# A decoder layer on one core: thirteen 8 KB buffers kept in one pool to the end, norm inputs fetched at step 60, and VectorE's hi and lo parts interleaved in the branch stage

## The chip, the cores and the metric

The kernel runs on one core of a Trainium2 chip. The metric is the device time of one execution in microseconds (us), as the median of several runs. TensorE (PE) multiplies, VectorE (DVE) and ScalarE (ACT) do elementwise work, GpSimd (POOL) does a little of it, and SyncE (SP) issues most DMAs.

## The reference

One decoder layer, on x of 512 tokens by 1024 channels, all in float32. Cut to what matters:

```python
proj = x @ w_in                       # q, k, v (3 groups x 8 heads x 64), ssm input, gate logits
q, k = apply_rope(q), apply_rope(k)
attn = merge of three windowed causal attentions, weighted by their softmax denominators
y_attn = attn @ w_attn_br
y_s = s5_ssm(u, ...)                  # complex diagonal state space model
glu = gelu(y_s) @ w_glu
y_ssm = (glu[:, :512] * sigmoid(glu[:, 512:])) @ w_ssm_br
mixed = sigmoid(gate0) * y_attn + sigmoid(gate1) * y_ssm
h = layer_norm(2 ** 0.25 * x + mixed @ w_out)
ff = (silu(h @ w_ff_gate) * (h @ w_ff_up)) @ w_ff_down
out = layer_norm(2 ** 0.25 * h + ff)
```

## The kernel before

Every product is made of three fp32r matmuls. An operand is split into a rounded part (hi) and the remainder (lo): `split` (line 177) has ScalarE copy the value into hi, and VectorE then subtract hi from the value to give lo. `mm3` (line 185) multiplies hi by hi, hi by lo and lo by hi (lines 186 to 188). Activations and weights are both split, each weight tile just in time.

Weights pass through the class `Weights`. SP loads units of 1 MB into two buffers `raw`; a unit holds two tiles, and `split` turns a tile into `whi` and `wlo`, three steps ahead of its use. `release`, called at the end of a step, gives that step's slot back and splits the next tile. The load of a unit is issued when the second tile of the unit two before it has been split. The second half of `w_out` (tiles 72 to 75) is not split into slots but into 8 KB buffers of its own, `w`.

The work is a list of numbered steps. Steps 0 to 55 project x and run the state space model and the attention in between (`at_step` hangs a function on a step number, `run_fill` calls it). Then come:

- GLU, steps 56 to 59: two banks of 12 matmuls each, then a tanh and a product, split into `gh`, `gl`.
- The branch stage, steps 60 to 67, counted n = 0 to 7 here: two banks per step, 24 matmuls. The banks come from a ring of four (0 to 3), so step n + 2 writes the banks that VectorE reads after step n. For n below 4 VectorE multiplies the state space branch by its gate (`gt`); from n = 4 it does so for the attention branch, adds both and splits the sum into `mix_hi`, `mix_lo`.
- `merge_pair(hp)`, at steps 58, 59, 60 and 61, for the four pairs of heads: two matmuls spread the merge weights to banks (`wb`), and VectorE forms `oa[1] * wb[1]`, then `a1 = oa[0] * wb[0]`, then their sum, which is split into `ath`, `atl`. In step 60 and 61 it stands ahead of the step's own gate products in VectorE's order. `oa[0]` is held in phase order, so that the product reads it with a stride of four elements.
- The output stage (`wo`): four token tiles by two column halves, eight weight tiles n. The first half goes over all four token tiles for each weight tile (banks 4 to 7), the second (banks 0 to 3) is done token tile by token tile. `wo_out` adds x (`xn`) and takes statistics; `normalize_shared` norms a token tile, half of its columns on VectorE and half on ScalarE and GpSimd; `turn_h` transposes it on TensorE (`hb`) and splits it into `hh`, `hl`. `turn_h(0)` stands in t = 2 after n = 5, `turn_h(1)` in t = 3 after n = 5.
- Feed forward (`fg`) and its last product (`dn`), then the second norm and the stores.

Two groups of 8 KB buffers are used. Pool `pa` has tags `big0` to `big8` and `gat0` to `gat3`, thirteen in all, given by name with `home`. It is closed after the branch stage (line 1031), together with the smaller `at` and `sa`; pool `pb` is opened over the same memory, with eleven buffers `ff` and a tile `hn`. The inputs of the norm, two halves of x (`xn`) and the scale and offset (`lnb`), 1 MB each, are loaded into `ff` buffers: `xn` at the start of the output stage, `lnb` after its second weight tile. Engines run their instructions in the order of the program, and so does SP.

Of the kernel before, what the change touches and what calls it, by code (L numbers as in the profile page):

```python
# [10 lines left out]
F32 = mybir.dt.float32  # L11
# [140 lines left out]
def emit(ctx, tc, i, out):  # L152
# [42 lines left out]
    def kslice(pair, k, cols=slice(None)):  # L195
        return pair[0][k // 4][:, k % 4, cols], pair[1][k // 4][:, k % 4, cols]

    pa_ctx = ExitStack()
    pa = pa_ctx.enter_context(tc.tile_pool(name="pa", bufs=1))
    at = pa_ctx.enter_context(tc.tile_pool(name="at", bufs=2))  # L200
    sa = pa_ctx.enter_context(tc.tile_pool(name="sa", bufs=1))

# [14 lines left out]
        return gat(n[1:], name, dt) if isinstance(n, str) else big(n, name, dt)  # L217

    w = Weights(nc, wp, split)
    w.add(None, 8)  # L220
    for n in range(2, N_GLU, 2):
        kind, g, un, _ = STEPS[n]
# [10 lines left out]
    for un in range(2):  # L233
        w.add(i["w_out"][un], 2)
    for un in range(2, 4):
        w.add(i["w_out"][un], 2, lambda name, dt: ffslot(name, dt))
    for f in range(NFF):
        w.add(i["w_gu"][f], 8)
    for f in range(NFF // 2):
# [32 lines left out]
    w.n_split = 4  # L272
    w.load()

    rope = pa.tile([P, 2, 512], F32, tag="rope", name="rope")
    masks = pa.tile([P, 512], F32, tag="masks", name="masks").rearrange("p (n k) -> p n k", n=2)
    bgate = sa.tile([P, 16], F32, name="bgate")
    prep = gat(0, "prep")
    sm = prep[:, 0:1024].rearrange("p (a r e) -> p a r e", a=2, r=2)
# [157 lines left out]
    powers(pw, lb)  # L437


    bb = pa.tile([P, 512], F32, tag="bb", name="bb").rearrange("p (r g h) -> p r g h", r=2, g=NGP)  # L440
    btmp = [zt[:, 256 * j : 256 * (j + 1)].rearrange("p (g h) -> p g h", g=NGP) for j in range(2)]
    b_raw = sm[:, 0].rearrange("p r (g h) -> p r g h", h=16)
    c_raw = sm[:, 1].rearrange("p r (g h) -> p r g h", h=16)
# [352 lines left out]
    def attn_values(kind, hp, blks):  # L796
        if blks[0] == 0:
            units["o", kind] = outs(f"o{kind}{hp}")
        ob = units["o", kind]
        for blk in blks:  # L800
            ks, tv = units.pop((kind, hp, blk))
            for c, (z, kb) in enumerate(ks):
                for hh in range(2):
                    h = 2 * hp + hh
                    pe.matmul(ob[64 * hh : 64 * hh + 64, 128 * blk : 128 * blk + 128],
                              z[2][:, kb, 64 * h : 64 * h + 64], tv[:, hh, 128 * c : 128 * c + 128],
                              start=(c == 0), stop=(c == len(ks) - 1))
        if blks[-1] == 3:
            if hp == 0:
                oa[kind] = big((6, 3)[kind], f"oa{kind}").rearrange("p (q t) -> p q t", q=4)  # L810
            act.copy(oa[kind][:, hp, :], ob)

    merged = {}

# [2 lines left out]
    def merge_near(n):  # L817

        if n == 0:
            merged["wt"] = wt = pa.tile([P, 512], F32R, tag="bb", name="wt").rearrange("p (r e) -> p r e", r=4)  # L820
            pool.memset(wt[:, :, 32:P].bitcast(F32), 0.0)
            sp.dma_start(sdr.rearrange("(b p) e -> p b e", p=P), st[0].rearrange("p b e h -> p b (e h)"))
        else:
            sp.dma_start(near_st.rearrange("p r e h -> p (r e h)"), sdr.rearrange("(c r) e -> c (r e)", r=4))

    def merge_sel():

        z = pa.tile([P, 2, 512], F32R, tag="rope", name="selr")
        for kind in range(2):
            hi, lo = (ident[:, c : c + 8].unsqueeze(2).broadcast_to([P, 8, 64]) for c in (8 * kind, 8 * kind + 16))  # L830
            tt(z[:, kind].rearrange("p (h m) -> p h m", m=64), hi, lo, ALU.add)
        merged["sel"] = z.rearrange("p k (h m) -> p k h m", h=NPAIR)
# [19 lines left out]
    def merge_turn():  # L852
        b = turned("wt")
        for r in range(4):
            pe.transpose(b[:, 128 * r : 128 * r + 128], merged["wt"][:, r].bitcast(F32), ident)

        merged["w"] = pa.tile([P, 512], F32R, tag="masks", name="whl")
        dve.tensor_copy(merged["w"], b)

    def merge_pair(hp):  # L860
        if hp == 0:
            for j, n in (("g1", "h"), (1, "l")):
                merged[n] = home(j, f"at{n}", F32R).rearrange("p (q t) -> p q t", q=4)
        wb = [pairs_(f"wb{hp}{k}") for k in range(2)]
        for kind in range(2):
            pe.matmul(wb[kind], merged["sel"][:, kind, hp, :], merged["w"], start=True, stop=True)
        tt(oa[1][:, hp, :], oa[1][:, hp, :], wb[1], ALU.mult)
        a1 = at.tile([P, 512], F32, tag="cq", name=f"a1{hp}")
        tt(by_phase(a1), as_phases(oa[0][:, hp, :]), by_phase(wb[0]), ALU.mult)
        tt(a1, a1, oa[1][:, hp, :], ALU.add)  # L870
        split(merged["h"][:, hp, :], merged["l"][:, hp, :], a1)

    gts = [None] * 4

# [61 lines left out]
    for kind in range(2):  # L936
        for j, n in enumerate(TURNS[kind]):
            if j >= 2:
                at_step(n, attn_values, kind, *pairs[j - 2])
            if j < len(pairs):  # L940
                at_step(n, attn_scores, kind, *pairs[j])
            if 0 < j <= len(pairs):
                at_step(n, attn_turn, kind, *pairs[j - 1])
    at_step(43, merge_near, 0)
    at_step(45, merge_near, 1)
    at_step(52, merge_sel)
# [38 lines left out]
    for n in range(4):  # L985
        ws = w.views[N_GLU + n]
        bs = []
        for e in range(2):
            b = glu(f"gl{n}{e}")
            co = slice(128 * e, 128 * e + 128)  # L990
            for k in range(4):
                mm3(b, (ws[0][:, k, co], ws[1][:, k, co]), (gluin["y"][0][:, k, :], gluin["y"][1][:, k, :]), k == 0, k == 3)
            bs.append(b)
        th = at.tile([P, 512], F32, tag="sw", name=f"th{n}")
        act.activation(th, bs[1], AF.Tanh, scale=0.5)
        stt(th, th, 1.0, bs[0], ALU.add, ALU.mult)
        split(gh_[:, n, :], gl_[:, n, :], th, 0.5)
        w.release()
        run_fill(N_GLU + n)
        run_fill(N_GLU + n + 0.5)  # L1000
# [3 lines left out]
    for n in range(8):  # L1004
# [11 lines left out]
        part(0, (3,))  # L1016
        run_fill(N_BR + n)
        part(1, (3,))
        for c in range(2):
            ch = 2 * (n % 4) + c  # L1020
            t0, t1 = gts[ch // 4][:, ch % 4, :], gts[2 + ch // 4][:, ch % 4, :]
            if n < 4:
                stt(t1, t1, 1.0, bs[c], ALU.add, ALU.mult)
            else:
                stt(t0, t0, 1.0, bs[c], ALU.add, ALU.mult)
                tt(t0, t0, t1, ALU.add)
                hi, lo = kslice(mx, ch)
                split(hi, lo, t0, 0.5)
        w.release()
        run_fill(N_BR + n + 0.5)  # L1030
    pa_ctx.close()
# [3 lines left out]
    bt = ctx.enter_context(tc.tile_pool(name="bt", bufs=2))  # L1035
    w.free.extend((pb, n) for n in range(3, 5))

    def ffslot(name, dt=F32):
        return pb.tile([P, 2048], dt, tag="ff", name=name, bufs=11)

    xn = [ffslot(f"xn{j}").rearrange("p (t d) -> p t d", t=2) for j in range(2)]
    lnb = ffslot("lnb").rearrange("p (e d) -> p e d", e=2)
    hn = pb.tile([P, NTT, D], F32, name="hn")
    epsb = bt.tile([P, 1], F32, name="epsb", bufs=1)
    pool.memset(epsb, -0.5)

# [29 lines left out]
        pool.tensor_tensor(z[:, hi], z[:, hi], ln[:, 1, hi], op=ALU.add)  # L1076

    bst1 = [bt.tile([P, 2, 6], F32, name=f"bsta{t}", bufs=1) for t in range(NTT)]
    hp_ = tuple([ffslot(f"h{n}{j}", F32R).rearrange("p (k t) -> p k t", k=4) for j in range(2)] for n in "hl")

    def wo_mm(d, n, t):
        ws = w.views[N_OUT + n]
# [3 lines left out]

    def wo_out(d, t, e):
        cs = slice(512 * e, 512 * e + 512)
        stt(hn[:, t, cs], xn[t // 2][:, t % 2, cs], ALPHA, d, ALU.mult, ALU.add)
        dve.bn_stats(bst1[t][:, e, :], hn[:, t, cs])  # L1090

    hturn = ring(4, 5, 6, 7)

    def turn_h(t):
        z = hn[:, t, :]
        tsl = slice(128 * t, 128 * t + 128)
        for j in range(2):
            b = hturn(f"hb{t}{j}")
# [2 lines left out]
                pe.transpose(b[:, 128 * e : 128 * e + 128], z[:, 128 * k : 128 * k + 128], ident)  # L1101
            split(hp_[0][j][:, :, tsl], hp_[1][j][:, :, tsl], b.rearrange("p (e c) -> p e c", e=4))

    for j in range(2):
        sp.dma_start(xn[j], i["x"].rearrange("(t p) d -> p t d", p=P)[:, 2 * j : 2 * j + 2, :])
    od = [bank(4 + t, f"wo0{t}") for t in range(NTT)]
    for n in range(4):
        for t in range(NTT):
            wo_mm(od[t], n, t)
        if n < 3:  # L1110
            w.release()
            if n < 2:
                w.split()
            if n == 1:
                sp.dma_start(lnb, i["ln1"].unsqueeze(0).broadcast_to([P, 2, D]))
    for t in range(NTT):
        wo_out(od[t], t, 0)
    od = [bank(t, f"wo1{t}") for t in range(NTT)]
# [2 lines left out]
    for t in range(NTT):  # L1121
        for n in range(4, 8):
            wo_mm(od[t], n, t)
            if t >= 2 and n == 5:
                turn_h(t - 2)
        if t == 3:
            normalize_shared(hn[:, 2, :], mvs[2], lnb)
        wo_out(od[t], t, 1)
        dve.bn_aggr(mvs[t][:, 0:2], bst1[t])
        rstd(mvs[t])  # L1130
        if t < 2:
            normalize_shared(hn[:, t, :], mvs[t], lnb)
            w.split()
    normalize(hn[:, 3, :], mvs[3], lnb)
    w.split()


# [10 lines left out]
    def ff_gate(f):  # L1148
        if f % 2 == 0:
            if f < 14:  # L1150
                slot = ffslot(f"ff{f // 2}", F32R)
                ffs.append(slot.rearrange("p (e c t) -> p e c t", e=2, c=2))
            else:
                slot = ap_.tile([P, 4, 512], F32R, tag="act", name=f"ff{f // 2}")
# [20 lines left out]
            w.release()  # L1175
        ff_gate(f)

    lnb2 = ffslot("lnb2").rearrange("p (e d) -> p e d", e=2)
    act.dma_start(lnb2, i["ln2"].unsqueeze(0).broadcast_to([P, 2, D]))
    out_rows = out.rearrange("(c r) d -> r c d", r=NTT)  # L1180

# [12 lines left out]
    for k in range(NFF - NLAST):  # L1194
# [1 line left out]
            for e, cs in enumerate(halves):  # L1196
                down(acc[t][e], k, t, cs, k == 0, t == NTT - 1 and k == NFF - NLAST - 1)
        w.release()
    end = hn[:, NTT - 1, :]
    for e, cs in enumerate(halves):  # L1200
        stt(end[:, cs], end[:, cs], ALPHA, acc[NTT - 1][e], ALU.mult, ALU.add)
    bsts = [bt.tile([P, 4, 6], F32, name=f"bstb{t}", bufs=1) for t in range(NTT)]
# [8 lines left out]
        dve.bn_stats(bsts[NTT - 1][:, q, :], end[:, quarters[q]])  # L1211

    for t in range(NTT - 1):
        z, bst, mv = hn[:, t, :], bsts[t], mvs[t]
        for e, cs in enumerate(halves):
            for k in range(NFF - NLAST, NFF):
                down(acc[t][e], k, t, cs, False, k == NFF - 1)
# [113 lines left out]
```

## Time and profile before

| | |
|---|---|
| time, median of 3 runs | 867.07 us (866.84 to 867.53) |
| the profiled execution: its own time | 867.58 us |
| its span in the trace | 865.8 us |
| TensorE matmul busy | 851.9 us, 98% |
| VectorE busy | 487.4 us, 56% |
| ScalarE busy | 291.7 us, 34% |
| GpSimd busy | 25.4 us, 3% |

The rows further down come from the profiled execution. All times in them count from the start of its span. A matmul's row gives the time it takes from start to end, but matmuls overlap, so that the distance between starts is what one costs. What lies outside the span is the difference of the profiled execution's two times. An idle time of an engine stands in brackets, with the work that ended it behind the arrow.

### The profile page before, as it was taken

Reading aid. Unit: us, or ns where it says so; the run is one execution under the profiler, and the core shown is the slowest. Engines: PE = TensorE matmul, PEld = TensorE weight load, DVE = VectorE, ACT = ScalarE, POOL = GpSimd, SP = SyncE. Lnnn points to the kernel's source line nnn. Section 1 sums busy time; section 2 is a strip of 40 time slices with the busy share of each in tenths; the row PEclk is TensorE's granted clock in tenths of the full one; section 3 lists DMA queues with packets and bytes.
Section 4 is the critical chain, followed back from the end, with each engine's and each line's share of the span. In section 5 each row is a group of like instructions: output and inputs, shape, how many; then the busy total and the mean of one; then the engine's idle time right before and its main releaser. Section 6 shows DMA issues by size and latency. Waiting matters only on the chain.

```text
span 865.8 us, 11316 instructions
## 1 busy us (share of the span) xinstructions
PE 851.9 (98%) x4586; PEld 701.7 (81%) x4586; DVE 487.4 (56%) x948; ACT 291.7 (34%) x475; POOL 25.4 (3%) x27
## 2 busy tenths in 40 slices
PE   9999999999999999999999899999999999999996
PEld 7878888887778888888788798888888888888885
DVE  7966899964666447247775864444444444222237
ACT  6364331154443254553233332222222222211101
POOL 0000000000000000000000500000000000000004
PEclk9999999999999999999999999999999999999998
DMA  9723421425121321121227132222222222322204
GB/s 351 174 84 104 122 98 49 145 75 172 50 98 50 100 98 50 49 98 49 97 93 296 50 115 97 94 95 95 95 99 95 95 98 97 144 97 97 98 0 98
DMA packets 24484, 90.06 MB, mean 104 GB/s; under 512 B 6384, under 2 KB 10992, under 8 KB 15344
## 3 DMA queue, kind: packets, MB, share of 16 engines
q1 hardware_dynamic: 22704, 86.59, 29.5%
q10 hardware_dynamic: 1728, 2.74, 0.9%
q8 instruction: 36, 0.59, 0.3%
q14 instruction: 16, 0.13, 0.0%
HBM read 84.87 MB, written 4.46 MB: 103 GB/s over the span
## 4 chain that ended last, share of the span: by engine, by line
PE 89%; DVE 6%; ACT 2%; DMA 1%; issue 1%; POOL 1%; DVEq 0%; POOLq 0%; ACTq 0%
PE fg L187 9%; PE fg L186 9%; PE fg L188 9%; PE dn L188 4%; PE dn L186 4%; PE dn L187 4%; PE pg L186 3%; PE pg L187 3%; PE pg L188 3%; PE pv L186 3%; PE pu L565 3%; PE pv L187 3%; PE pk L186 3%; PE pv L188 3%; PE pq L186 3%; PE pk L187 3%
## 5 line engine op out<-in xcount | busy, mean ns | idle before, releaser
L180 DVE TENSOR_TENSOR wlo<-raw,whi 128x1024 fp32r<-128x1024 f32 x134 | 164.3, 1227 | 198.9 <-ACT whi L179 198.7
L179 ACT CAST whi<-raw 128x1024 fp32r<-128x1024 f32 x134 | 140.1, 1047 | 222.5 <-PE dn L188 73.3
L187 PE MATMUL fg<-hl,whi 128*128 128x512 f32 (+1 forms) x376 | 141.3, 376 | 0.3 <-DVE hl L180 0.3
L186 PE MATMUL fg<-hh,whi 128*128 128x512 f32 (+1 forms) x376 | 141.4, 376 | 0.2 <-ACT hh L179 0.2
L188 PE MATMUL fg<-hh,wlo 128*128 128x512 f32 (+1 forms) x376 | 141.2, 375 | 0.0
L187 PEld LDWEIGHTS fg<-hl,whi 128*128 128x128 f32 x376 | 70.8, 188 | 13.3 <-DVE hl L180 0.5
L186 PEld LDWEIGHTS fg<-hh,whi 128*128 128x128 f32 x376 | 70.8, 188 | 13.2 <-ACT hh L179 0.5
L188 PEld LDWEIGHTS fg<-hh,wlo 128*128 128x128 f32 x376 | 70.8, 188 | 12.9
L186 PE MATMUL dn<-whi,ff 128*128 128x512 f32 x168 | 65.4, 389 | 0.0
L187 PE MATMUL dn<-wlo,ff 128*128 128x512 f32 x168 | 65.4, 389 | 0.0
L188 PE MATMUL dn<-whi,ff 128*128 128x512 f32 x168 | 65.4, 389 | 0.0
L186 PE MATMUL pg<-x_hi,whi 128*128 128x512 f32 x128 | 50.6, 396 | 0.0
L187 PE MATMUL pg<-x_lo,whi 128*128 128x512 f32 x128 | 49.9, 390 | 0.0
L188 PE MATMUL pg<-x_hi,wlo 128*128 128x512 f32 x128 | 49.9, 390 | 0.0
L182 ACT ACTIVATE ff<-fth 128x512 fp32r<-128x512 f32 x22 | 14.0, 635 | 102.7 <-DVE fth L309 102.7
L309 DVE TENSOR_TENSOR fth<-fth,fg 128x512 f32<-128x512 f32 x22 | 15.1, 687 | 56.9 <-PE fg L188 56.8
L779 ACT ACTIVATE pt<-pt,st 128x256 f32<-128x256 f32 (+1 forms) x64 | 31.0, 485 | 42.0 <-DVE st L777 42.0
L186 PE MATMUL pk<-x_hi,whi 128*128 128x512 f32 x96 | 37.8, 394 | 0.0
L186 PE MATMUL pq<-x_hi,whi 128*128 128x512 f32 x96 | 37.8, 394 | 0.0
L188 PE MATMUL pk<-x_hi,wlo 128*128 128x512 f32 x96 | 37.4, 390 | 0.0
L188 PE MATMUL pq<-x_hi,wlo 128*128 128x512 f32 x96 | 37.4, 390 | 0.0
L187 PE MATMUL pq<-x_lo,whi 128*128 128x512 f32 x96 | 37.4, 389 | 0.0
(254 smaller groups left out, 1465.9 us busy)
## 6 DMA issues: line engine op xcount, KB each, us to landing
raw<-in_w_in SPq DMA_DIRECT2D x26, 1024.0 KB, 4.8
raw<-in_w_gu SPq DMA_DIRECT2D x22, 1024.0 KB, 4.7
raw<-in_w_dn SPq DMA_DIRECT2D x11, 1024.0 KB, 4.7
raw<-in_w_br SPq DMA_DIRECT2D x4, 1024.0 KB, 4.7
raw<-in_w_out SPq DMA_DIRECT2D x4, 1024.0 KB, 4.8
raw<-in_w_glu SPq DMA_DIRECT2D x2, 1024.0 KB, 4.8
xn<-in_x SPq DMA_DIRECT2D x2, 1024.0 KB, 5.9
out_dram<-hn SPq DMA_DIRECT2D x13, 128.0 KB, 2.4
```

The lines of the kernel that those rows point to most:

```text
L179: act.copy(hi, src)
L180: dve.tensor_tensor(lo, src, hi.bitcast(F32), op=ALU.subtract)
L182: act.mul(hi, src, scale)
L186: pe.matmul(dst, a[0], b[0], start=first, stop=False)
L187: pe.matmul(dst, a[0], b[1], start=False, stop=False)
L188: pe.matmul(dst, a[1], b[0], start=False, stop=last)
L309: eng.tensor_tensor(o, a, b, op=op)
L565: pe.matmul(bs[e], wk[a], xk[b], start=(k + a + b == 0), stop=(k == KT - 1 and a == 1))
L779: act.activation(pt[:, :n], pt[:, :n], AF.Exp, bias=mneg, scale=-1.0, accum_out=zsum)
```

## The change

The pool `pa` stays open to the end of the kernel, and the buffers that `ff` gave are now taken from it by name. The rope table, masks and merge weights move to a small pool `pr`, which is closed with `at` and `sa`; `pb` now holds only two weight slots. `load_norm` loads `xn` and `lnb` at step 60.5. `merge_pair` and the branch stage no longer call `split` but let ScalarE make hi and do other VectorE work ahead of lo. `oa[0]` is put into token order by ScalarE's copy of it, four times, which now reads PSUM with a stride. `turn_h(0)` moves by one weight tile.

```diff
@@ pools @@
+    pa = ctx.enter_context(tc.tile_pool(name="pa", bufs=1))
     pa_ctx = ExitStack()
-    pa = pa_ctx.enter_context(tc.tile_pool(name="pa", bufs=1))
+    pr = pa_ctx.enter_context(tc.tile_pool(name="pr", bufs=1))
...
+    out_homes = deque(("g0", 2, 6, 3))
...
-        w.add(i["w_out"][un], 2, lambda name, dt: ffslot(name, dt))
+        w.add(i["w_out"][un], 2, lambda name, dt: home(out_homes.popleft(), name, dt))
@@ attn_values @@
-            act.copy(oa[kind][:, hp, :], ob)
+            if kind == 0:
+                act.copy(by_phase(oa[kind][:, hp, :]), as_phases(ob))
+            else:
+                act.copy(oa[kind][:, hp, :], ob)
@@ merge_pair @@
-        tt(by_phase(a1), as_phases(oa[0][:, hp, :]), by_phase(wb[0]), ALU.mult)
+        tt(a1, oa[0][:, hp, :], wb[0], ALU.mult)
         tt(a1, a1, oa[1][:, hp, :], ALU.add)
-        split(merged["h"][:, hp, :], merged["l"][:, hp, :], a1)
+        hi, lo = merged["h"][:, hp, :], merged["l"][:, hp, :]
+        act.copy(hi, a1)
+        pending.append(lambda: tt(lo, a1, hi.bitcast(F32), ALU.subtract))
@@ new @@
+    def load_norm():
+        for j, h in enumerate((0, "g3")):
+            xn.append(home(h, f"xn{j}").rearrange("p (t d) -> p t d", t=2))
+            sp.dma_start(xn[j], i["x"].rearrange("(t p) d -> p t d", p=P)[:, 2 * j : 2 * j + 2, :])
+        xn.append(home("g2", "lnb").rearrange("p (e d) -> p e d", e=2))
+        sp.dma_start(xn[2], i["ln1"].unsqueeze(0).broadcast_to([P, 2, D]))
+
+    def flush():
+        while pending:
+            pending.pop(0)()
+
+    at_step(60.5, load_norm)
@@ GLU @@
         stt(th, th, 1.0, bs[0], ALU.add, ALU.mult)
+        flush()
         split(gh_[:, n, :], gl_[:, n, :], th, 0.5)
@@ branch stage @@
+        for c, (ch, t0, t1) in enumerate(ts_):
             if n < 4:
                 stt(t1, t1, 1.0, bs[c], ALU.add, ALU.mult)
             else:
                 stt(t0, t0, 1.0, bs[c], ALU.add, ALU.mult)
                 tt(t0, t0, t1, ALU.add)
+                act.mul(kslice(mx, ch)[0], t0, 0.5)
+        flush()
+        if n >= 4:
+            for ch, t0, _ in ts_:
                 hi, lo = kslice(mx, ch)
-                split(hi, lo, t0, 0.5)
+                stt(lo, t0, 0.5, hi.bitcast(F32), ALU.mult, ALU.subtract)
@@ output stage @@
-    xn = [ffslot(f"xn{j}").rearrange("p (t d) -> p t d", t=2) for j in range(2)]
-    lnb = ffslot("lnb").rearrange("p (e d) -> p e d", e=2)
-    hn = pb.tile([P, NTT, D], F32, name="hn")
+    lnb = xn[2]
+    hns = [home(4 + j, f"hn{j}").rearrange("p (t d) -> p t d", t=2) for j in range(2)]
...
-    for j in range(2):
-        sp.dma_start(xn[j], i["x"].rearrange("(t p) d -> p t d", p=P)[:, 2 * j : 2 * j + 2, :])
...
-            if n == 1:
-                sp.dma_start(lnb, i["ln1"].unsqueeze(0).broadcast_to([P, 2, D]))
...
-            if t >= 2 and n == 5:
+            if n == (None, None, 6, 5)[t]:
                 turn_h(t - 2)
```

The tiles `hh` now lie in `big7` and `big8`, `hl` in `gat1` and `big1`, the products `ff0` to `ff6` in `big0`, `gat3`, `gat0`, `big2`, `big6`, `big3` and `gat2`, and the second norm's `lnb2` in `big7`.

## Rows read from the trace of the kernel before

**Rows 1.** The page, busy time and share of the span.

```profile
PE 851.9 (98%) x4586; PEld 701.7 (81%) x4586; DVE 487.4 (56%) x948; ACT 291.7 (34%) x475; POOL 25.4 (3%) x27
```

**Rows 2.** Waits of TensorE: us in total, times, longest.

```profile
PE hb L1101 <- POOL hn L1076: 2.2, 1, 2.2
PE b L186 <- DVE gt L306: 1.7, 2, 1.4
```

**Rows 3.** Timeline of TensorE, branch stage: start, us, instruction, idle before.

```profile
399.98 0.39 PE L186 MATMUL b<-gh,whi 128*128 128x512 f32 x1
...
413.30 0.47 PE L186 MATMUL b<-gh,whi 128*128 128x512 f32 x1 [1.38 <-DVE gt L306]
...
419.30 0.47 PE L186 MATMUL b<-gh,whi 128*128 128x512 f32 x1 [0.28 <-DVE gt L306]
...
424.86 0.39 PE L186 MATMUL b<-ath,whi 128*128 128x512 f32 x1
```

**Rows 4.** Timeline of VectorE, merges of pairs 1 to 3 and the gates.

```profile
405.12 0.68 DVE L309 TENSOR_TENSOR oa<-oa,wb 128x512 f32<-128x512 f32 x1
405.72 1.05 DVE L309 TENSOR_TENSOR a<-oa,wb 128x512 f32<-128x512 f32 x1
406.81 0.69 DVE L309 TENSOR_TENSOR a<-a,oa 128x512 f32<-128x512 f32 x1
408.19 0.69 DVE L180 TENSOR_TENSOR atl<-a,ath 128x512 fp32r<-128x512 f32 x1 [0.69 <-ACT ath L179]
...
412.48 1.28 DVE L306 SCALAR_TENSOR_TENSOR gt<-gt,b 128x512 f32<-128x512 f32 x2
...
418.48 1.28 DVE L306 SCALAR_TENSOR_TENSOR gt<-gt,b 128x512 f32<-128x512 f32 x2
```

**Rows 5.** Groups by line: ScalarE's copies, busy, mean ns, idle before.

```profile
L811 ACT COPY oa<-o 128x512 f32<-128x512 f32 x8 | 4.7, 585 | 1.1 <-PE o L805 1.1
...
L727 ACT COPY vt<-pv 128x512 f32<-128x512 f32 x4 | 4.3, 1084 | 9.4 <-PE pv L188 9.4
```

**Rows 6.** Timeline of TensorE, second half of the output stage.

```profile
468.40 0.39 PE L186 MATMUL wo<-w,mix_hi 128*128 128x512 f32 x1
...
482.01 0.60 PE L1101 MATMUL hb<-ident,hn 128*128 128x128 f32 x4
484.82 0.66 PE L1101 MATMUL hb<-ident,hn 128*128 128x128 f32 x4 [2.22 <-POOL hn L1076]
485.24 0.48 PE L186 MATMUL wo<-w,mix_hi 128*128 128x512 f32 x1
...
490.80 1.04 PE L1101 MATMUL hb<-ident,hn 128*128 128x128 f32 x8
491.60 0.47 PE L186 MATMUL wo<-w,mix_hi 128*128 128x512 f32 x1
```

**Rows 7.** Timeline of VectorE, output stage.

```profile
468.56 2.36 DVE L180 TENSOR_TENSOR w<-raw,w 128x1024 fp32r<-128x1024 f32 x2 [7.63 <-ACT w L179]
...
477.24 0.68 DVE L306 SCALAR_TENSOR_TENSOR hn<-xn,wo 128x512 f32<-128x512 f32 x1
...
483.57 0.68 DVE L306 SCALAR_TENSOR_TENSOR hn<-xn,wo 128x512 f32<-128x512 f32 x1
```

**Rows 8.** Timeline of GpSimd, the norm of token tiles 0 and 1.

```profile
481.27 1.29 POOL L1075 TENSOR_TENSOR hn<-hn,lnb 128x512 f32<-128x512 f32 x1 [1.12 <-ACT hn L1074]
482.64 2.13 POOL L1076 TENSOR_TENSOR hn<-hn,lnb 128x512 f32<-128x512 f32 x1
...
488.98 2.16 POOL L1076 TENSOR_TENSOR hn<-hn,lnb 128x512 f32<-128x512 f32 x1
```

**Rows 9.** SP's issues at the start of the output stage.

```profile
456.14 0.89 SPq L1105 DMA_DIRECT2D xn<-in_x  x2
```

**Rows 10.** The chain that ended last, in order of time: start, us, what.

```profile
458.69 8.77 DMA raw<-in_w_out
```

**Rows 11.** The page, DMA issues: KB each, median us to landing.

```profile
raw<-in_w_out SPq DMA_DIRECT2D x4, 1024.0 KB, 4.8
```

More of the change, by code (lines that the diff above doesn't have):

```diff
@@ L273, in emit @@
     w.load()
-    rope = pa.tile([P, 2, 512], F32, tag="rope", name="rope")
-    masks = pa.tile([P, 512], F32, tag="masks", name="masks").rearrange("p (n k) -> p n k", n=2)
+    rope = pr.tile([P, 2, 512], F32, tag="rope", name="rope")
+    masks = pr.tile([P, 512], F32, tag="masks", name="masks").rearrange("p (n k) -> p n k", n=2)
     bgate = sa.tile([P, 16], F32, name="bgate")
@@ L437, in emit @@
     powers(pw, lb)
-    bb = pa.tile([P, 512], F32, tag="bb", name="bb").rearrange("p (r g h) -> p r g h", r=2, g=NGP)
+    bb = pr.tile([P, 512], F32, tag="bb", name="bb").rearrange("p (r g h) -> p r g h", r=2, g=NGP)
     btmp = [zt[:, 256 * j : 256 * (j + 1)].rearrange("p (g h) -> p g h", g=NGP) for j in range(2)]
@@ L819, in merge_near @@
         if n == 0:
-            merged["wt"] = wt = pa.tile([P, 512], F32R, tag="bb", name="wt").rearrange("p (r e) -> p r e", r=4)
+            merged["wt"] = wt = pr.tile([P, 512], F32R, tag="bb", name="wt").rearrange("p (r e) -> p r e", r=4)
             pool.memset(wt[:, :, 32:P].bitcast(F32), 0.0)
@@ L826, in merge_sel @@
     def merge_sel():
-        z = pa.tile([P, 2, 512], F32R, tag="rope", name="selr")
+        z = pr.tile([P, 2, 512], F32R, tag="rope", name="selr")
         for kind in range(2):
@@ L855, in merge_turn @@
             pe.transpose(b[:, 128 * r : 128 * r + 128], merged["wt"][:, r].bitcast(F32), ident)
-        merged["w"] = pa.tile([P, 512], F32R, tag="masks", name="whl")
+        merged["w"] = pr.tile([P, 512], F32R, tag="masks", name="whl")
         dve.tensor_copy(merged["w"], b)
@@ L943, in emit @@
                 at_step(n, attn_turn, kind, *pairs[j - 1])
+    xn = []
+    pending = []
+    def load_norm():
[8 more added lines that the diff above has]
+    at_step(60.5, load_norm)
     at_step(43, merge_near, 0)
@@ L1018, in emit @@
         part(1, (3,))
-        for c in range(2):
-            ch = 2 * (n % 4) + c
-            t0, t1 = gts[ch // 4][:, ch % 4, :], gts[2 + ch // 4][:, ch % 4, :]
+        ts_ = [(2 * (n % 4) + c, *(gts[2 * j + n % 4 // 2][:, (2 * n + c) % 4, :] for j in range(2))) for c in range(2)]
+        for c, (ch, t0, t1) in enumerate(ts_):
             if n < 4:
@@ L1036, in emit @@
     w.free.extend((pb, n) for n in range(3, 5))
-    def ffslot(name, dt=F32):
-        return pb.tile([P, 2048], dt, tag="ff", name=name, bufs=11)
-    xn = [ffslot(f"xn{j}").rearrange("p (t d) -> p t d", t=2) for j in range(2)]
-    lnb = ffslot("lnb").rearrange("p (e d) -> p e d", e=2)
-    hn = pb.tile([P, NTT, D], F32, name="hn")
+    lnb = xn[2]
+    hns = [home(4 + j, f"hn{j}").rearrange("p (t d) -> p t d", t=2) for j in range(2)]
+    hn = [hns[t // 2][:, t % 2, :] for t in range(NTT)]
     epsb = bt.tile([P, 1], F32, name="epsb", bufs=1)
@@ L1078, in emit @@
     bst1 = [bt.tile([P, 2, 6], F32, name=f"bsta{t}", bufs=1) for t in range(NTT)]
-    hp_ = tuple([ffslot(f"h{n}{j}", F32R).rearrange("p (k t) -> p k t", k=4) for j in range(2)] for n in "hl")
+    hp_ = tuple([home(h, f"h{n}{j}", F32R).rearrange("p (k t) -> p k t", k=4) for j, h in enumerate(hs)] for n, hs in (("h", (7, 8)), ("l", ("g1", 1))))
     def wo_mm(d, n, t):
@@ L1088, in wo_out @@
         cs = slice(512 * e, 512 * e + 512)
-        stt(hn[:, t, cs], xn[t // 2][:, t % 2, cs], ALPHA, d, ALU.mult, ALU.add)
-        dve.bn_stats(bst1[t][:, e, :], hn[:, t, cs])
+        stt(hn[t][:, cs], xn[t // 2][:, t % 2, cs], ALPHA, d, ALU.mult, ALU.add)
+        dve.bn_stats(bst1[t][:, e, :], hn[t][:, cs])
     hturn = ring(4, 5, 6, 7)
     def turn_h(t):
-        z = hn[:, t, :]
+        z = hn[t]
         tsl = slice(128 * t, 128 * t + 128)
@@ L1123, in emit @@
             wo_mm(od[t], n, t)
-            if t >= 2 and n == 5:
+            if n == (None, None, 6, 5)[t]:
                 turn_h(t - 2)
         if t == 3:
-            normalize_shared(hn[:, 2, :], mvs[2], lnb)
+            normalize_shared(hn[2], mvs[2], lnb)
         wo_out(od[t], t, 1)
@@ L1131, in emit @@
         if t < 2:
-            normalize_shared(hn[:, t, :], mvs[t], lnb)
+            normalize_shared(hn[t], mvs[t], lnb)
             w.split()
-    normalize(hn[:, 3, :], mvs[3], lnb)
+    normalize(hn[3], mvs[3], lnb)
     w.split()
@@ L1150, in ff_gate @@
             if f < 14:
-                slot = ffslot(f"ff{f // 2}", F32R)
+                slot = home((0, "g3", "g0", 2, 6, 3, "g2")[f // 2], f"ff{f // 2}", F32R)
                 ffs.append(slot.rearrange("p (e c t) -> p e c t", e=2, c=2))
@@ L1176, in emit @@
         ff_gate(f)
-    lnb2 = ffslot("lnb2").rearrange("p (e d) -> p e d", e=2)
+    lnb2 = home(7, "lnb2").rearrange("p (e d) -> p e d", e=2)
     act.dma_start(lnb2, i["ln2"].unsqueeze(0).broadcast_to([P, 2, D]))
@@ L1198, in emit @@
         w.release()
-    end = hn[:, NTT - 1, :]
+    end = hn[NTT - 1]
     for e, cs in enumerate(halves):
@@ L1213, in emit @@
     for t in range(NTT - 1):
-        z, bst, mv = hn[:, t, :], bsts[t], mvs[t]
+        z, bst, mv = hn[t], bsts[t], mvs[t]
         for e, cs in enumerate(halves):
```

## The prediction

> **What bounds the kernel now.** I read the page's busy times first: TensorE is busy for 851.9 of 865.8 us [rows 1]. The change takes no matmul away, so what it can give is TensorE's idle time alone, and of that only what lies near the edited code. The waits of TensorE come second. Two of them lie there: a transposition in the output stage waited once, 2.2 us, for GpSimd's norm, and matmuls of the branch stage waited twice, 1.7 us together, for VectorE's gate product [rows 2]. Third, the timelines of each place, to see who is late and why.
>
> In the branch stage [rows 3] the reader is to see two matmuls of a new step that find their bank not yet read, at 413.30 and 419.30. What they cost is more than the idle time. From the first matmul of n = 0 at 399.98 to the first of n = 4 at 424.86 there are 96 matmuls and 4 of the merges, in 24.88 us. Without waits 60 such matmuls take 13.61 us, 468.40 to 482.01 [rows 6], 0.227 each; 100 take 22.68. So the stage loses 2.20 us, the idle 1.66 and a slower restart after each. Who is late is VectorE [rows 4]: the gate of n = 0, done by TensorE before 406, is read only at 412.48, since two merges stand ahead of it, and the gate of n = 1 at 418.48 for the same reason.
>
> In the output stage [rows 6] the eight transpositions of token tile 0 start at 482.01 and the next matmul at 485.24, 3.23 us; those of tile 1 take 0.80 from 490.80 to 491.60. So 2.43 us are lost. The cause goes back further: the halves of x are issued at 456.14 [rows 9], ahead of the load of weight tiles 74 and 75, which is issued at 458.69 and lands 8.77 us later [rows 10], where such a load takes 4.8 [rows 11]. VectorE sits idle for 7.63 us until ScalarE has split what came, ends these splits at 470.92, and comes to token tile 0's second half at 477.24 [rows 7], though TensorE finished it after 24 matmuls from 468.40, at 473.84 and about 0.2 for its end. From 477.24 it is a chain without slack to GpSimd's last add, 482.64 + 2.13 = 484.77 [rows 8].
>
> **The change, part by part.** *Merges.* A merge now takes VectorE 0.60 for the first product, 1.09 for the second with its strided read, 0.69 for the sum (to 407.5), a wait of 0.69 and 0.61 for lo, 3.68 in all (405.12 to the next at 408.80) [rows 4]. Without the stride the second product is like the first, 0.60, and with lo put off a merge takes 0.60 + 0.60 + 0.70 = 1.90. The merges of pairs 1 and 2 then end at 405.12 + 3.80 = 408.92 at the latest, and the first gate of n = 0 at 409.6. TensorE wants that bank after 48 matmuls and two merges, 52 x 0.227 = 11.8 us after 399.98, at 411.8: 2.2 us of slack, where it was 1.5 us late. For n = 1: the two gates (1.2), two lo parts (1.3), a weight split (1.2), merge 3 (1.9) and a gate (0.6) end at 408.92 + 6.2 = 415.1, wanted at 411.8 + 5.4 = 417.2. Both waits go: **2.20 us**. The lo parts put off come well before n = 4 reads them.
>
> *ScalarE's strided copies.* No row shows ScalarE reading PSUM with a stride. Bounds: 0.585 as now, and 1.084 as for the copy that writes with a stride [rows 5], so 0 to 0.5 us more for each of four. I take the upper end, the nearer row, and cost it at nothing: the copies lie in the attention stage, where no wait of TensorE for ScalarE stands among the two long ones. Without that cover it is 2.0 us. The Trainium skill, in "Advanced Engine Details and Errata", section "PSUM Cachelines", says that PSUM reads want pairs of neighbouring elements and that other patterns slow matmuls significantly; it gives no figure for ScalarE, and no row here shows one. By it the upper end would hold, and with no cover at all the time would be 864.4.
>
> *hi and lo from n = 4.* Eight short waits of VectorE go, behind which TensorE does not wait. Nothing.
>
> *Loads.* Three issues move from 456 to after step 60, behind one weight load, with GLU's buffers free since 400. Three MB more at 4.8 us for one [rows 11] is at most 14.4 us in which weight loads share. Those are for tiles 66 to 69, needed from 435 on; the first load lands by about 430 even then. Nothing. In the output stage the load issued at 458.69 lands after 4.8, at 463.5. The splits end 3.46 after landing (467.46 to 470.92), at 466.95. From there VectorE needs what it needed from 470.92 to 477.24, 6.32, so 473.3; TensorE gives the tile at 474.1, and this comes last now. The chain starts 3.1 us earlier.
>
> *turn_h(0) one tile later* is 6 matmuls, 1.36 us, of cover. The second four transpositions are reached at 482.01 + 1.36 + 0.4 = 483.8 and the norm ends at 484.77 - 3.1 = 481.7: 2.1 us of slack. **2.43 us** go. Token tile 1: the chain of 483.57 [rows 7] also starts 3.1 earlier, and its last add ends at 491.14 - 3.1 = 488.0 [rows 8]. TensorE is there after 24 matmuls and 12 transpositions' time of tile 0 and 1, 482.01 + 5.45 + 0.8 + 0.4 = 488.7: slack 0.7. This is what is late next, if anything.
>
> *Buffers by name.* They are taken after their last readers in the same order as before. No cost; the waits that the old pool's closing could bring are the SP issue just counted.
>
> Here a page speaks against the change. A GpSimd add took 2.13 and 2.16 us, the multiply just before it 1.29, same shape [rows 8]; the longer ones lie beside a weight split on VectorE. The Trainium skill, "SBUF — State Buffer", section "Who interferes with whom", has VectorE and GpSimd lock each other out when a VectorE instruction with two SBUF inputs meets a GpSimd read: the one that starts second waits for the whole of the other. The trace agrees (2.13 against 1.29). The norm keeps its place among VectorE's instructions, so I leave the adds as they are.
>
> **Sum.** 2.20 + 2.43 = 4.63 us. The profiled execution's 867.58 would become 862.95; the median of the runs is 0.51 below it, 867.07, so **862.4**.
>
> **Rivals.** *A: the norm is late all the same.* If VectorE comes to tile 0 as late as now, the norm ends at 484.77 and TensorE, there at 483.8, loses 1.0, then at tile 1 another 1.4 (491.14 against 489.7): 2.4 of 4.63 given back, 864.8. For it: VectorE's queue is long there. Against it: its 7.63 us idle. In a mild form, the multiply also meets a split, 0.84 more on tile 1's chain: 0.14 past its slack, 862.6, within my range. Such a meeting is the page's rule just named.
>
> *B: the branch waits stay.* The gates would have to come 2.2 us later than worked out; then 2.43 alone, 864.6. Against it: the order of the program puts only known instructions ahead.
>
> *C: given back.* TensorE, 4.6 us earlier, meets VectorE in the first feed forward tiles and waits there, 867.1. Against it: VectorE's whole output stage moves 3.1 earlier, TensorE's only 2.4.
>
> *D: slower.* SP issues in order; the three loads wait for three named buffers, and behind them stand the weight loads. If a buffer came free late, the load of tiles 68 and 69, needed at 446.6 and taking 4.8 and some 2.3 to split, has slack until 439.5; each us beyond is lost. It decides from 439.5 + 4.6 = 444.1, and at 447 the time is 870. Against it: the last readers of these buffers end by 400.
>
> **How the numbers follow.** Forecast (both waits gone, up to 1 us of new ones, 861.7 to 863.5) 0.72; A 0.12; B 0.06; C 0.07; D 0.03. The range of 8 in 10 takes in A and B: 861.7 to 865.0. A measurement of this kernel can tell about 0.2%, 1.7 us: under 865.3 is faster, so 0.72 + 0.12 + 0.06 = 0.90; C is the same, 0.07; D slower, 0.03.
>
> **What would show it.** Right: the branch stage's n = 0 to n = 4 takes 22.7 us with no wait for a gate; the gate of n = 0 within 4.6 us of the merge of pair 1; no wait of the transpositions for GpSimd; the `w_out` load lands in about 4.8 us; VectorE at tile 0's second half right behind TensorE. Wrong: a wait at token tile 1's transpositions, GpSimd adds above 2.2 us, or a new TensorE wait for ScalarE in the attention stage.

## The result and the profile after

The changed kernel takes 862.60 us (median of 6 runs, 862.37 to 862.97), the kernel before in the same runs 867.02. The ratio is 0.9948, its 95% interval 0.9935 to 0.9960: 4.4 us faster, 0.2 us from the forecast of 862.4. The profiled execution took 862.37 us with a span of 860.6. The page's busy times say that TensorE did the same work with less idle time, 860.6 - 850.2 = 10.4 us where it was 13.9 [rows 1]:

```profile
PE 850.2 (99%) x4586; PEld 701.4 (82%) x4586; DVE 485.9 (56%) x948; ACT 291.7 (34%) x475; POOL 25.4 (3%) x27
```

The waits of TensorE (us in total, times, longest) no longer name a gate or GpSimd; the two of [rows 2] are gone. This is all of them; the one of `pu`, which the kernel before does not have, stands at 5.19 us, far ahead of step 56:

```profile
PE warm_b L262 <- DVE warm L258: 1.1, 1, 1.1
PE tv L736 <- ACT pmT L514: 0.3, 1, 0.3
PE fg L187 <- DVE hl L180: 0.3, 1, 0.3
PE pu L568 <- DVE wuh L467: 0.3, 1, 0.3
PE fg L186 <- ACT hh L179: 0.2, 1, 0.2
```

The timeline of TensorE shows n = 0 and n = 4 of the branch stage (first two rows, against [rows 3]), the start of the second half of the output stage, the transpositions of token tiles 0 and 1 with the matmuls that follow them (against [rows 6]), and the first full feed forward matmul:

```profile
399.40 0.39 PE L186 MATMUL b<-gh,whi 128*128 128x512 f32 x1
...
422.06 0.39 PE L186 MATMUL b<-ath,whi 128*128 128x512 f32 x1
...
465.58 0.39 PE L186 MATMUL wo<-w,mix_hi 128*128 128x512 f32 x1
...
480.55 1.03 PE L1125 MATMUL hb<-ident,hn 128*128 128x128 f32 x8
481.34 0.48 PE L186 MATMUL wo<-w,mix_hi 128*128 128x512 f32 x1
...
485.52 1.04 PE L1125 MATMUL hb<-ident,hn 128*128 128x128 f32 x8
486.32 0.47 PE L186 MATMUL wo<-w,mix_hi 128*128 128x512 f32 x1
...
509.28 0.40 PE L186 MATMUL fg<-hh,whi 128*128 128x512 f32 x1
```

From n = 0 to n = 4 it is 22.66 us, where it was 24.88: 2.22 gone, 2.20 forecast. The transpositions of tile 0 now take 0.79 us where they took 3.23: 2.44 gone, 2.43 forecast. The two profiled spans differ by 5.2 us; the other 0.58 lies ahead of step 60 (399.40 against 399.98). Of the edits only ScalarE's copies, the new pools and the merges of pairs 0 and 1 stand there. Step 60 starts at 399.24 in `e10` and at 400.44 in `e3`, both with the old merges and copies and with the new pools, so I count the 0.58 as spread between executions. The medians differ by 4.4.

VectorE's timeline shows why the first wait went (against [rows 4]): the merge of pair 1, the merge of pair 2 right behind it, and the gate at 407.91 instead of 412.48. The next gate comes at 413.37 instead of 418.48:

```profile
404.07 0.68 DVE L312 TENSOR_TENSOR oa<-oa,wb 128x512 f32<-128x512 f32 x1
404.66 0.68 DVE L312 TENSOR_TENSOR a<-oa,wb 128x512 f32<-128x512 f32 x1
405.38 0.69 DVE L312 TENSOR_TENSOR a<-a,oa 128x512 f32<-128x512 f32 x1
405.99 0.68 DVE L312 TENSOR_TENSOR oa<-oa,wb 128x512 f32<-128x512 f32 x1
...
407.91 1.28 DVE L309 SCALAR_TENSOR_TENSOR gt<-gt,b 128x512 f32<-128x512 f32 x2
...
413.37 1.28 DVE L309 SCALAR_TENSOR_TENSOR gt<-gt,b 128x512 f32<-128x512 f32 x2
```

A merge takes 404.07 to 405.99, 1.92 us, where 1.90 was worked out. Further on in the same timeline, against [rows 7], VectorE has ended the splits of tiles 72 to 75 at 458.51, and then waits for TensorE's first output until 461.70 (the second row), not the other way round. In the third row it comes to token tile 0's second half right behind TensorE (465.58 + 5.44 = 471.02):

```profile
456.15 2.36 DVE L180 TENSOR_TENSOR w<-raw,w 128x1024 fp32r<-128x1024 f32 x2 [3.57 <-ACT w L179]
461.70 0.69 DVE L309 SCALAR_TENSOR_TENSOR hn<-xn,wo 128x512 f32<-128x512 f32 x1 [3.19 <-PE wo L188]
...
471.22 0.69 DVE L309 SCALAR_TENSOR_TENSOR hn<-xn,wo 128x512 f32<-128x512 f32 x1 [2.90 <-PE wo L188]
...
477.64 0.68 DVE L309 SCALAR_TENSOR_TENSOR hn<-xn,wo 128x512 f32<-128x512 f32 x1
```

GpSimd's last adds (against [rows 8]) end at 478.87 and 485.20. TensorE reaches the second four transpositions at about 480.97 and 485.94, so the slack is 2.1 and 0.7 us, as worked out, and the adds take what they took:

```profile
476.71 2.16 POOL L1100 TENSOR_TENSOR hn<-hn,lnb 128x512 f32<-128x512 f32 x1
...
483.04 2.16 POOL L1100 TENSOR_TENSOR hn<-hn,lnb 128x512 f32<-128x512 f32 x1
```

And the group of ScalarE's copies that now read PSUM with a stride, against [rows 5]:

```profile
L815 ACT COPY oa<-o 128x512 f32<-128x512 f32 x4 | 2.3, 587 | 0.9 <-PE o L808 0.9
```

### The profile page after: what moved, and what is told of

Its sections match the earlier page's. It is cut to its first block, busy times and chain, and to the rows that moved or that the text cites. A ratio compares the mean times of both kernels' runs of the same rounds, so it can differ in the third digit from the quotient of the medians.

```text
span 860.6 us, 11311 instructions
## 1 busy us (share of the span) xinstructions
PE 850.2 (99%) x4586; PEld 701.4 (82%) x4586; DVE 485.9 (56%) x948; ACT 291.7 (34%) x475; POOL 25.4 (3%) x27
## 4 chain that ended last, share of the span: by engine, by line
PE 98%; DVE 0%; DMA 0%; ACT 0%; issue 0%; DVEq 0%
PE fg L188 9%; PE fg L187 9%; PE fg L186 9%; PE dn L188 4%; PE dn L187 4%; PE dn L186 4%; PE pg L186 3%; PE pg L187 3%; PE pg L188 3%; PE pv L186 3%; PE pu L568 3%; PE pv L187 3%; PE pk L186 3%; PE pv L188 3%; PE pq L186 3%; PE pk L188 3%
```

## The experiments

The sum came out; what the experiments have to tell is which of the edits earned it. The theory, from the prediction: the merges earn 2.2 us in the branch stage, the earlier loads earn 2.4 in the output stage, and the rest nothing. The rivals: the edits earn each other's share, or several of them cure the same wait. Most experiments undo one edit, or do one alone. They ran in three groups, each with the kernel before beside it, whose median was 867.22 to 867.40 there and 867.02 beside the changed kernel. So a difference of some 0.4 us from the changed kernel's median says nothing, and what small waits cost is read from the traces.

**The merges, undone and alone.** In `e3` the changed kernel has the old merges and the old copy of `oa[0]` (not shown):

```diff
-        tt(a1, oa[0][:, hp, :], wb[0], ALU.mult)
+        tt(by_phase(a1), as_phases(oa[0][:, hp, :]), by_phase(wb[0]), ALU.mult)
...
-        act.copy(hi, a1)
-        pending.append(lambda: tt(lo, a1, hi.bitcast(F32), ALU.subtract))
+        split(merged["h"][:, hp, :], merged["l"][:, hp, :], a1)
```

> The changed kernel, with merge_pair and the copy of oa as before (strided product, lo right behind hi). Theory: the merges alone caused the branch stage's waits for the gate, so the 2.2 us come back there and nothing else does: 864.8 us, 2.2 above the changed kernel's 862.6, with two waits of the branch matmuls for VectorE's gate of 1.4 and 0.3 us, and no wait of the transpositions. Rival: the early loads or the other edits had cured the branch stage; then 862.6 and no such wait.

It took 864.77 us, 2.2 above the changed kernel. Its waits have the gate's line back, equal to that of [rows 2], and no transposition waits:

```profile
PE b L186 <- DVE gt L309: 1.7, 2, 1.4
```

In `e8` the kernel before has the new merges, and nothing else of the change.

> The kernel before, with the edits of merge_pair alone (ScalarE puts oa into token order, lo put off). Theory: the branch stage's 2.2 us go, the transposition's wait of 2.2 us for GpSimd stays: 864.8 us against 867.0. Rival: VectorE, earlier in the branch stage, is earlier in the output stage too, and the second wait shrinks as well: 862.6 to 864.

It took 866.29 us (864.87 to 867.01, 12 runs), not 864.8, ratio 0.9985 (0.9976 to 0.9993). The branch stage did what was expected: 399.52 to 422.19, 22.67 us, no wait there. The transposition's wait stayed, at 1.94 us shorter than before [rows 6], but it cost more. TensorE's timeline of that place:

```profile
481.86 1.00 PE L1114 MATMUL hb<-ident,hn 128*128 128x128 f32 x4 [1.94 <-POOL hn L1089]
482.51 0.78 PE L186 MATMUL wo<-w,mix_hi 128*128 128x512 f32 x1
483.08 0.63 PE L187 MATMUL wo<-w,mix_hi 128*128 128x512 f32 x1
483.51 0.63 PE L188 MATMUL wo<-w,mix_lo 128*128 128x512 f32 x1
...
485.55 0.39 PE L187 MATMUL wo<-w,mix_hi 128*128 128x512 f32 x1
485.78 0.39 PE L188 MATMUL wo<-w,mix_lo 128*128 128x512 f32 x1
```

Behind the wait matmuls stand 0.43 us apart until 485.2, and then 0.23 again. The row of the 5 us around it (busy time of each engine, then the granted clock) shows that the clock fell; in the part of it from 483 to 485 the granted clock is 0.50, the lower level of 1.2 GHz:

```profile
480.00:485.00 5.00, 3.14 (x10) 2.67 (x11) 3.81 (x8) 1.27 (x2) 3.17 (x3) 0.70 0.59 211
```

From the transpositions of tile 0 (479.31) to those of tile 1 (489.43) it is 10.12 us, where the kernel before takes 8.79 [rows 6]. Those 1.33 us are nearly all that is missing (866.29 against 864.8). The runs agree: three of the twelve have a mean granted clock of 0.998 and took 864.87 to 865.40, nearly what was expected; the other nine, at 0.994 to 0.996, took 865.84 to 867.01. The kernel before varies in the same way: of its 18 runs beside these, four have 0.995 or 0.996 and took 868.24 to 869.46, the other fourteen took 866.49 to 867.72. Like against like, the mean is 865.15 against 867.07 at the higher clock and 866.43 against 868.83 at the lower, 1.9 and 2.4 us. So the merges are worth about their 2.2 us, and the wait that stays has a price that varies from run to run. Where in the other runs the clock fell no trace shows.

**What of the merges counts.** `e5` keeps ScalarE's copies into token order and splits at once; `e6` puts lo off and keeps the strided product and the old copy (not shown):

```diff
@@ e5 @@
-        act.copy(hi, a1)
-        pending.append(lambda: tt(lo, a1, hi.bitcast(F32), ALU.subtract))
+        split(merged["h"][:, hp, :], merged["l"][:, hp, :], a1)
@@ e6 @@
-        tt(a1, oa[0][:, hp, :], wb[0], ALU.mult)
+        tt(by_phase(a1), as_phases(oa[0][:, hp, :]), by_phase(wb[0]), ALU.mult)
```

> The changed kernel, with lo right behind hi in merge_pair (ScalarE still puts oa into token order). Theory, by the prediction's merge sums: a merge takes 3.19 instead of 1.90 us of VectorE, the gate of n = 0 ends at 412.1 against 411.8 wanted, that of n = 1 at about 417.6 against 417.2: short waits, 0.5 to 1.2 us lost, 863.1 to 863.8. Rival: the stride was the whole matter: 862.6.

> The changed kernel, with the strided product of oa as before (lo still put off). Theory: a merge takes 2.39 us, the gate of n = 0 ends 1.3 us and that of n = 1 0.6 us before TensorE wants them: no wait, 862.6 us. Rival: the waits return in part, 863.1 or more.

`e5` took 863.25 us, 0.65 above the changed kernel's median, but equal to it by the ratio to the kernel before (0.9947 against 0.9948), so the time alone does not tell. The trace does: there is one wait for the gate (timeline of TensorE), and the branch stage from n = 0 to n = 4 takes 23.40 us (399.38 to 422.78), 0.74 more than in the changed kernel:

```profile
411.59 0.47 PE L186 MATMUL b<-gh,whi 128*128 128x512 f32 x1 [0.26 <-DVE gt L309]
```

`e6` took 862.77 us with no such wait, 22.67 us in the branch stage. Putting lo off is enough by itself. Without it the contiguous product removes most of the loss, not all.

**The loads.** `e10` is the kernel before with named buffers alone, all loads in their old place; `e2` is the changed kernel with the loads back in their old place:

```diff
@@ e2 @@
-    at_step(60.5, load_norm)
...
-    lnb = xn[2]
+    load_norm()
+    lnb = home("g2", "lnb").rearrange("p (e d) -> p e d", e=2)
...
+            if n == 1:
+                sp.dma_start(lnb, i["ln1"].unsqueeze(0).broadcast_to([P, 2, D]))
```

Of `load_norm` only the two loads of x are left in it.

> The kernel before, with the buffers kept in one pool and given by name alone; loads of x and lnb at their old place in the program, merges, interleaving and turn_h as before. Theory: it is the closing of the pool that held the loads of x until VectorE's last lo (456), so by name they go out at once behind the load before them, at about 451, the next w_out load lands within about 6 us, and the transposition's wait goes: 864.6 us. Rival: the place in the program is what matters (step 60.5), then they still collide and the time is 866 to 867.

> The changed kernel, with the loads of x and lnb issued at their old places in the program (into the same named buffers). Theory: not held by a closing pool, they go out behind the load for tiles 72 and 73, at about 445, and the one for 74 and 75 lands at most 2 us later than in the changed kernel, of which VectorE has 3 us to spare before the first wo_out: 862.6 us. Rival: they collide with the weight loads as before and the transposition waits 1 to 2.4 us: 863.6 to 865.

`e10` took 864.74 us, `e2` 862.37. In neither does a transposition wait. SP's issues in `e10`, against [rows 9]:

```profile
450.27 0.94 SPq L953 DMA_DIRECT2D xn<-in_x  x2
457.93 0.34 SPq L116 DMA_DIRECT2D raw<-in_w_out  x1
```

The loads of x go out 5.9 us earlier from the same place in the program (5.1, counted from the start of step 60), right behind the weight load before them: nothing but the closing of the old pool had held them. The `w_out` load goes out when it did before and still takes 6.4 us (ScalarE splits it from 464.39), not 4.8 but not 8.8 either, and that is enough. The step at which the loads stand earns nothing more beside the other edits: `e2` is as fast as the changed kernel.

**hi and lo from n = 4.** `e7` is the kernel before with this edit alone, `e4` the changed kernel without it:

```diff
@@ e4; e7 the other way round @@
-                act.mul(kslice(mx, ch)[0], t0, 0.5)
...
-                stt(lo, t0, 0.5, hi.bitcast(F32), ALU.mult, ALU.subtract)
+                split(hi, lo, t0, 0.5)
```

> The kernel before, with hi and lo interleaved from n = 4 on alone. By the prediction's step this is worth nothing: 867.0 us. Rival, seen since in the changed kernel's trace (VectorE's last lo there is about 5 us earlier): the old pool closes when VectorE's last lo is done, so the loads of x start about 4.5 us earlier, the load of tiles 74 and 75 lands by about 462 instead of 467.5, and the norm's chain starts behind TensorE: the transposition's wait goes and the time is 864.6, the branch waits of 1.7 us staying.

> The changed kernel, with hi and lo as before from n = 4 on. Theory: VectorE's last lo is 4 to 5 us later, which with the x loads already done moves the load of tiles 74 and 75 from about 451 to about 455, landing at about 460 and split by 464; TensorE gives the first output at about 462: 862.6 us. Rival: the interleaving is needed for the output stage by itself: 1 to 2.4 us more.

`e4` took 863.01 us (862.13 to 863.18), 0.4 above the changed kernel, by the ratio to the kernel before 0.9938 against 0.9948: there the edit is worth nothing that these runs resolve. What it gives there is room. Without it VectorE comes to tile 0's second half at 472.48 with no wait for TensorE; in the changed kernel it has waited 2.90 us. `e7` took 865.04, 2.2 below the kernel before (ratio 0.9971, 0.9960 to 0.9982), without a transposition's wait. The prediction's "nothing" is wrong for this edit alone. SP's issues in `e7`:

```profile
450.79 0.89 SPq L1107 DMA_DIRECT2D xn<-in_x  x2
453.35 0.34 SPq L116 DMA_DIRECT2D raw<-in_w_out  x1
```

VectorE's last lo of the branch stage, first in the kernel before and then in `e7`:

```profile
455.36 0.69 DVE L183 SCALAR_TENSOR_TENSOR mix_lo<-gt,mix_hi 128x512 fp32r<-128x512 f32 x1 [0.70 <-ACT mix_hi L182]
```

```profile
449.24 1.47 DVE L306 SCALAR_TENSOR_TENSOR mix_lo<-gt,mix_hi 128x512 fp32r<-128x512 f32 x2
```

It ends at 456.05 and the loads of x go out at 456.14 [rows 9]; in `e7` it ends at 450.71 and they go out at 450.79. That is the pool's closing at work. The wait that goes is the one that `e10` cures, but by another way. In `e7` the `w_out` load still stands right behind the loads of x and takes 7.3 us (ScalarE splits it from 460.63); it goes out 5.3 us earlier, since VectorE, which no longer waits for each hi, ends the weight split that the load follows at 453.32 and not at 458.66.

**turn_h(0).** `e9` is the kernel before with the later transposition alone, `e1` the changed kernel with the old place:

```diff
@@ e1; e9 the other way round @@
-            if n == (None, None, 6, 5)[t]:
+            if t >= 2 and n == 5:
```

> The kernel before, with turn_h(0) one weight tile later alone. Theory (rival A of the prediction worked out): 1.0 us is lost at token tile 0 and 1.4 at token tile 1, together the 2.4 us of before: 867.0. Rival: the later place covers 1.36 us for good: 865.7.

> The changed kernel, with turn_h(0) behind n = 5 as before. Theory: the norm of token tile 0 ends 0.8 us before TensorE reaches its second four transpositions even so: 862.6 us, no wait there. Rival: the move is needed, and up to 1.4 us comes back: 863.5 to 864.

`e9` took 867.38 us against 867.36, `e1` 862.53: nothing in either. In `e9` the wait only changes its place, 0.64 us at tile 0 and 1.10 at tile 1 (timeline of TensorE), as rival A had it:

```profile
484.03 0.66 PE L1101 MATMUL hb<-ident,hn 128*128 128x128 f32 x4 [0.64 <-POOL hn L1076]
...
490.35 0.66 PE L1101 MATMUL hb<-ident,hn 128*128 128x128 f32 x4 [1.10 <-POOL hn L1076]
```

**The price of a wait.** `e12` is the changed kernel with `turn_h(0)` ahead of token tile 2's matmuls, so that it must wait:

```diff
+        if t == 2:
+            turn_h(0)
         for n in range(4, 8):
             wo_mm(od[t], n, t)
-            if n == (None, None, 6, 5)[t]:
-                turn_h(t - 2)
+            if t == 3 and n == 5:
+                turn_h(1)
```

> The changed kernel, with turn_h(0) ahead of token tile 2's matmuls, three weight tiles (4.1 us) earlier. It measures what a wait there costs. Theory: the second four transpositions are reached 2.0 us before the norm ends, so the wait is 2.0 and the time 864.7 if TensorE's granted clock stays at its upper level, and 865.5 to 866.5 in runs in which it falls behind the wait, as the trace of the kernel with the merge edits alone shows (0.70 granted in the 5 us with a wait of 1.9). Rival: a wait costs its length and no more, all runs at 864.7.

It took 864.69 us, all five runs between 864.48 and 864.85: 2.1 us for a wait of 1.82, and no fall of the clock. The wait, and the row of the 4 us around it (granted clock 1.00):

```profile
479.00 0.66 PE L1125 MATMUL hb<-ident,hn 128*128 128x128 f32 x4 [1.82 <-POOL hn L1100]
```

```profile
478.00:482.00 4.00, 3.00 (x15) 2.57 (x16) 2.97 (x7) 1.11 (x2) 2.16 (x3) 1.00 0.73 260
```

So an idle stretch of nearly the same length as that of `e8` left the clock alone. What decides it stays open.

**A version that beats both.** The changed kernel's waits name one more pair near the edits: the feed forward matmuls behind the last transposition wait 0.24 and 0.34 us for its split. `e11` moves `turn_h(3)` into the middle of the feed forward tile ahead of them:

```diff
-    def ff_mm(f, e, cs):
+    def ff_mm(f, e, cs, mid=None):
...
         for k in range(KT):
+            if k == 4 and mid:
+                mid()
...
-        ff_mm(n // 2, n % 2, slice(0, 256))
-        if n > 0:
-            turn_h(1 + n)
+        ff_mm(n // 2, n % 2, slice(0, 256), (lambda: turn_h(3)) if n == 2 else None)
+        if n == 1:
+            turn_h(2)
```

> The changed kernel, with turn_h(3) in the middle of the third feed forward tile instead of behind it, so that 12 half matmuls, 1.4 us, cover ScalarE's and VectorE's split of the last transposition, for which TensorE waits 0.24 and 0.34 us now. Theory: 0.6 to 0.8 us gained, 861.9. Rival: the norm of token tile 3 is then late and nothing is gained, 862.6 or more.

It took 861.33 us (861.12 to 861.54), ratio to the kernel before 0.9923 (0.9909 to 0.9937). Of its waits only two are left, both in the first steps:

```profile
PE warm_b L262 <- DVE warm L258: 1.1, 1, 1.1
PE tv L736 <- ACT pmT L514: 0.3, 1, 0.3
```

Its timeline of TensorE has the start of the output stage's second half and the first full feed forward matmul:

```profile
465.92 0.39 PE L186 MATMUL wo<-w,mix_hi 128*128 128x512 f32 x1
...
508.50 0.40 PE L186 MATMUL fg<-hh,whi 128*128 128x512 f32 x1
```

Between them lie 42.58 us, in the changed kernel 43.70: 1.12 us gained for 0.58 of idle time. The idle time understates the loss, since the modelled end of a transposition or matmul lies past the start that its successor would have had. The distance of starts tells it.

## Why the prediction was right

*What bounds the kernel* held: the gain that the traces place is TensorE's idle time at the two places named, and no new wait came up near the edits.

*Merges, 2.20 us*: right in size (2.22 in the trace, 2.2 by `e3`) and in mechanism. The gate of n = 0 was forecast to end at 409.6 at the latest and ends at about 408.5. Of the two parts, putting lo off suffices (`e6`); the contiguous product by itself leaves 0.74 us of the loss (`e5`).

*ScalarE's strided copies*: costed at nothing by their cover. No cover was needed: they take 0.587 us, where the plain ones took 0.585. Of the two bounds I took the wrong one, without effect on the sum.

*Loads, 2.43 us with turn_h*: right in size, and from VectorE's waiting for TensorE on the chain ran as worked out, down to the slack of 2.1 and 0.7 us. Ahead of that it did not. The sum left the issue of the `w_out` load at 458.69 and shortened its way alone, which put VectorE 0.8 us ahead of TensorE at tile 0's second half. In the changed kernel the load goes out 8.3 us earlier, of which step 60's start and the branch stage give 2.8 and the hi and lo edit most of the rest (5.3 in `e7`). SP's issue:

```profile
450.34 0.33 SPq L116 DMA_DIRECT2D raw<-in_w_out  x1
```

VectorE was 2.90 us ahead. Since TensorE came last either way, the size did not change, and that is partly luck. In `e4`, without the hi and lo edit, the load took 5.9 us and not 4.8 (issued at 456.77, split from 462.72), VectorE came some 0.4 us behind TensorE (472.48 against about 472.1), and of the slack of 0.7 us at tile 1's transpositions 0.4 was left (the add ended at 486.43, TensorE is there at about 486.83).

The step that was credited is not the one that counts, either. What held the loads of x was the pool's closing, which waited for VectorE's last lo. Naming the buffers lets them go out ahead (`e10`), an earlier lo brings them and the weight load forward together (`e7`), and with both in place the move to step 60.5 adds nothing (`e2`). The third of the loads that were said to move from 456, that of `lnb`, stood at 461.35; the sum does not use it. The prediction's "no cost" for the names and "nothing" for hi and lo from n = 4 miss this: each of the two edits alone takes the wait away, 2.5 us by `e10` and 2.2 by `e7`, and beside each other they earn it once.

*turn_h(0)*: the slack without its move was worked out as 2.1 - 1.36, 0.7 us, and `e1` shows that the move is not needed; `e9` shows that alone it only shifts the wait, rival A's sum.

*Rivals*: A came in no part, and the mild form of it with GpSimd's multiply did not either: multiply and add kept their lengths. B was refuted by the branch stage's 22.66 us, C by the lack of any new wait in the feed forward part (the two of `fg`, 0.3 and 0.2, are in the kernel before too), D by SP's issue of the loads at 411.94, right behind one weight load:

```profile
411.94 0.94 SPq L958 DMA_DIRECT2D xn<-in_x  x2
```

What the prediction left out is that the price of the output stage's wait was not one number. It was worked out for the profiled execution, in which the clock held (granted 1.00 from 480 to 490).

## What to carry to other kernels

A pool that is closed and reopened over the same memory ties the first load of the new pool to the last work on the old one (0.09 and 0.08 us behind it in the kernel before and in `e7`); look at what SP's first issue behind it waited for before moving the issue in the program. Before adding up gains of edits, ask which of them cure the same wait: here two edits each cure one wait of 2.4 us alone, and beside each other earn it once. Where TensorE waits for VectorE, count what lies ahead of the bank's reader in VectorE's order, and move out the parts that nobody needs yet.

## What the runs showed of the hardware

ScalarE's copy of 128x512 out of PSUM with a stride of four elements took 0.587 us against 0.585 without; the copy that writes SBUF with a stride takes 1.084 [rows 5], and VectorE's product that read SBUF with the stride 1.05 against 0.68. The Trainium skill, "Advanced Engine Details and Errata", section "PSUM Cachelines", speaks of matmuls slowed by such patterns; for ScalarE's reads nothing of the kind shows here.

A wait of TensorE of 1.94 us was followed in the trace of `e8` by some 3 us at the lower clock, which added 1.3 us; one of 2.22 us in the trace of the kernel before and one of 1.82 in that of `e12` were not.
